# Five PSUM banks for the expert combines, and the last expert's rows taken out one expert earlier, in an encoder layer with 16 experts

## The chip, the cores and the metric

The kernel runs on one core of a Trainium2 chip. The metric is device time in microseconds for one execution of the whole layer. Before: 973.5 us, the median of three runs (973.33 to 974.92).

Five engines work beside each other, each in its own order: TensorE (matmuls; PE in the profile, and PEld for its weight loads), VectorE (DVE), ScalarE (ACT), GpSimd (POOL) and SyncE (SP), which issues nearly all transfers. TensorE writes into PSUM, which has eight banks; a 128x512 float32 tile fills one.

## What is computed

One encoder layer on 512 tokens of width 1024. Three attention branches, gated and merged, give `x` after a first layer norm. The change touches only what follows:

```python
    logits = jnp.einsum('btd,de->bte', x, w_router, preferred_element_type=jnp.float32)
    aff = jax.nn.softmax(logits, axis=-1)
    gate, idx = lax.top_k(jnp.swapaxes(aff, 1, 2), cap)          # 16 experts, cap = 64 tokens each
    xs = x[bidx, idx]
    h = jnp.einsum('becd,edf->becf', xs, w_gate_up)              # 1024 -> 2 x 1024
    hg, hu = jnp.split(h, 2, axis=-1)
    ye = jnp.einsum('becf,efd->becd', jax.nn.silu(hg) * hu, w_down)
    ye = ye * gate[..., None].astype(ye.dtype)
    ffn = jnp.zeros_like(x).at[bidx, idx].add(ye)
    x = layer_norm(DN_ALPHA * x + ffn, ln2_g[l], ln2_b[l])
```

Each expert picks 64 of the 512 tokens; a token can be picked by several experts, and the layer norm of a token needs the sum of all of them.

## The kernel before

**Weights.** An expert has 8 slots of gate and up weights, written gu(e,k), and 4 slots of down weights, dn(e,k), each 1 MiB. `Ring` fixes their order: gu(e,0..3), dn(e-1,0..3), gu(e,4..7), and for the last two experts gu(e,0), dn(e-1,0..3), gu(e,1..7); dn(15,0..3) comes last. SyncE issues a slot's transfer (L783; L781 for a tag of two separate tiles, and for the last slot) as soon as a buffer is free; with 24 buffers some 20 MiB can lie ahead of TensorE. A few buffers aren't reused late in the stage (`ONCE`, `LEAVE`).

**One expert.** `gate_up` (L1212) multiplies the 64 gathered tokens by a slot: two halves of g and two of u, 8 matmul records of 128x512 a slot. g and u fill a PSUM bank each, of the tags S and T, which have two banks each. `act_h` computes h from them: a tanh on ScalarE (L1220), two products on VectorE (L1221, L1222). `h_transpose` turns h with four transposes (L1228) and a copy (L1231), `products` (L1240) multiplies by the four dn slots, 32 matmul records, into the one bank of the tag Y, and `hi_lo` splits the result (L86 on ScalarE, L87 on VectorE). The order is written out by hand in the loop over `e` at the end: while expert e's gu slots run, expert e-1 is transposed and multiplied. After an odd expert `gather` collects the tokens of the next two.

**The accumulator.** `acc_of(m)` holds the sum for token tile m (128 tokens, m = 0 to 3) in SBUF. `combine(pr)` adds the two experts of pair pr: per tile and half of the width a pair of matmuls with the one-hot matrix (L1317, L1318) into one of the three banks of the tag mm, and an addition on VectorE (L1325); the third and sixth are first copied out by ScalarE (L1322) and added later (L1311). It runs within experts 3, 5, ..., 13 and, for pair 6, within expert 14, seven times.

**The last two experts.** Within expert 15, `Rows` handles expert 14. `slots` (L1389) makes its one-hot matrix, `down` its products, and `combine(m)` adds them to tile m (L1403, L1405) and takes the row sums along; a mean on GpSimd (L1407) and squares on ScalarE (L1409) follow. `take(m)` (L1413) then picks the rows that expert 15 needs out of the finished accumulator into a bank `fin`, of the tag S. `centre` (L1417), `spread` (L1420, L1421), the reciprocal square root (L94, L95, L99 to L101) and `finish` (L1426, L1427) normalise all rows on VectorE and send them out. Expert 15's own products go into `fin` on top of the taken rows, and `last_rows` normalises these 64 rows (two halves of the width on 128 partitions) and sends them with an indirect transfer (L1449) over the rows that were written before. `last_own` works out, in expert 14, which rows these are (L1365 and L1368 on VectorE, L1372 on TensorE, L1374).

`keep_warm(n)` issues n matmuls whose result nobody reads. `PB(tag, name)` gives the next bank of a tag.

Of the kernel before, what the change touches and what calls it, by code (L numbers as in the profile page):

```python
# [18 lines left out]
P = 128  # L19
# [23 lines left out]
def layer_kernel(ctx: ExitStack, tc: tile.TileContext, xt, xn, first0, wu, bgate, rpb, gains, wrt,  # L43
# [14 lines left out]
    def R(tag, shape, name, dt=F32, bufs=None):  # L58
        return rp.tile(shape, dt, name=name, tag=tag, bufs=bufs)

    PS_BUFS = {"mm": 3, "S": 2, "T": 2, "Y": 1}

    class Halves:
        def __init__(self, a, b):
# [11 lines left out]
    def RH(tag, name, dt=F32R):  # L76
        return Halves(*(R(tag + c, [P, 4, S], name + c, dt) for c in "ab"))

    def PB(tag, name, shape=(P, 512)):
        return ps.tile(list(shape), F32, name=name, tag=tag, bufs=PS_BUFS[tag])  # L80

    def small(shape, name, dt=F32, bufs=2):
# [620 lines left out]
    class Attn:  # L703
# [4 lines left out]
        def add(self, us):  # L708
            self.units += us
# [353 lines left out]
    def all_of(g):  # L1063
        for _ in g:
            pass
# [1 line left out]
    def then(*fs):  # L1067
        return lambda: [f() for f in fs]

    def keep_warm(n):  # L1070
        warm2 = PB("T", "warm2")
        for _ in range(n):
            nc.tensor.matmul(warm2[:, :P], ident, ident, start=True, stop=True)

# [128 lines left out]
    def gate_up(e, ks):  # L1203
        pr, i = divmod(e, 2)
        if ks[0] == 0:
            GU[e] = (PB("S", f"g{e}"), PB("T", f"u{e}"))
        for k in ks:
            w = ring.get("gu", e, k)
            xs = XS[pr][:, k, i * CAP:(i + 1) * CAP]
            for b in range(2):  # L1210
                for hf in range(2):
                    nc.tensor.matmul(GU[e][b][hf * 64:hf * 64 + 64], xs,  # L1212
                                     w[b][:, hf * 512:hf * 512 + 512],
                                     start=(k == 0), stop=(k == KD - 1))
            ring.done("gu", e, k)

    def act_h(e):
        g, u = GU.pop(e)
        HT[e] = th = R("t", [P, 512], f"h{e}")
        nc.scalar.activation(th, g, AF.Tanh, scale=0.5)  # L1220
        nc.vector.scalar_tensor_tensor(th, th, 1.0, g, op0=ALU.add, op1=ALU.mult)  # L1221
        nc.vector.scalar_tensor_tensor(th, th, GW[e // 2][:, e % 2:e % 2 + 1], u, op0=ALU.mult, op1=ALU.mult)  # L1222

    def h_transpose(e):
        h = HT[e]
        tp = PB("mm", f"ht{e}", (P, 4, P))
        for c in range(4):
            nc.tensor.transpose(tp[:, c], h[:, c * P:(c + 1) * P], ident)  # L1228
        t = R("tmp", [P, 4, P], f"hT{e}", bufs=2)
        HT[e] = t  # L1230
        nc.vector.tensor_copy(t, tp)  # L1231

    def products(e, y, first):
        hT = HT.pop(e)
# [66 lines left out]
                    yield  # L1301
            yield

    def combine(pr):
        yh, yl = YP.pop(pr)
        g = GT.pop(pr)
        later = []

        def catch_up():
            a, t = later.pop()  # L1310
            nc.vector.tensor_tensor(a, a, t, op=ALU.add)  # L1311

        for i in range(2 * NT):
            m, o = divmod(i, 2)
            c = slice(o * 512, (o + 1) * 512)
            cb = PB("mm", f"cb{pr}{m}{o}")
            nc.tensor.matmul(cb, g[:, m], yh[:, c], start=True, stop=False)  # L1317
            nc.tensor.matmul(cb, g[:, m], yl[:, c], start=False, stop=True)  # L1318
            a = acc_of(m)[:, c]
            if i in (2, 5):  # L1320
                t = R("t", [P, 512], f"cbs{pr}{i}")
                nc.scalar.copy(t, cb)  # L1322
                later.append((a, t))
            else:
                nc.vector.tensor_tensor(a, a, cb, op=ALU.add)  # L1325
            if i == 3:
                catch_up()
        catch_up()

    E = NEXP - 1  # L1330
    HALVES = [(slice(o * 64, o * 64 + 64), slice(o * 512, o * 512 + 512)) for o in range(2)]
# [31 lines left out]
    def last_own():  # L1363
        own, half, base = OH[E // 2][:, :, CAP:], ST["half"], ST["base"]
        nc.vector.tensor_copy(ST["pick"], own)  # L1365
        code = late_small(2, F16)
        for m in range(NT):
            nc.vector.tensor_scalar(code[:, m:m + 1], base, 8.0, 2.0 * m - 8.0, op0=ALU.mult, op1=ALU.add)  # L1368
        at = PB("mm", "rowat")
        for r, _ in HALVES:  # L1370
            for m in range(NT):
                nc.tensor.matmul(at[r, :1], own[:, m], code[:, m:m + 1], start=(m == 0), stop=(m == NT - 1))  # L1372
        ST["rowat"] = late_small(1, I32)
        nc.vector.tensor_tensor(ST["rowat"], at[:, :1], half, op=ALU.add)  # L1374

    class Rows:
# [6 lines left out]
        def slots(self):  # L1383
# [6 lines left out]
            self.g = R("tmp", [P, NT, P], "GTe", F32R, bufs=2)  # L1390
            nc.scalar.copy(self.g, gp)

        def down(self):
            y = PB("Y", f"y{E - 1}")
            products(E - 1, y, True)
            self.yy = R("lo", [P, 2, D], "ye", F32R)[:, 0]
            for r, c in HALVES:
                hi_lo(self.yy[0:64, c], self.yy[64:128, c], y[r])

        def combine(self, m):  # L1400
            for o, (_, c) in enumerate(HALVES):
                cb = PB("mm", f"cbe{m}{o}")
                nc.tensor.matmul(cb, self.g[:, m], self.yy[:, c], start=True, stop=True)  # L1403
                a = acc_of(m)[:, c]
                nc.vector.scalar_tensor_tensor(a, a, 1.0, cb, op0=ALU.mult, op1=ALU.add, accum_out=self.sums[:, o, m:m + 1])  # L1405
            nm = self.nm[:, m:m + 1]
            nc.gpsimd.tensor_scalar(nm, self.sums[:, 0, m:m + 1], self.sums[:, 1, m:m + 1], -1.0 / D, op0=ALU.add, op1=ALU.mult)  # L1407
            for o, (_, c) in enumerate(HALVES):
                nc.scalar.activation(ST["junk"], acc_of(m)[:, c], AF.Square, bias=nm, accum_out=self.sq[:, o, m:m + 1])  # L1409

# [17 lines left out]

    def last_rows():
        fin = ST["fin"]  # L1430
        t, d = PB("T", "lastst")[:, :2], PB("Y", "lastd")[:, :1]
        nc.tensor.matmul(t, ST["pair"], ST["eps2"], start=True, stop=False)
        products(E, fin, False)
        st, mv = late_small(6), late_small(2)
# [22 lines left out]
    for e in range(NEXP):  # L1457
# [5 lines left out]
        elif e < NEXP - 2:  # L1463
# [4 lines left out]
            for k in range(4):  # L1468
                if k == 3:
                    h_transpose(e - 1)  # L1470
                    if e % 2 and e > 1:
                        combine((e - 3) // 2)
                gate_up(e, (k,))
                steps(side, side)
            if e == 12:
# [10 lines left out]
        elif e == NEXP - 2:  # L1486
            gate_up(e, (0,))
            h_transpose(e - 1)
            down(e - 1)
            rows = Rows()  # L1490
            rows.slots()
            last_own()
            gate_up(e, (1, 2))
            combine(e // 2 - 1)
            gate_up(e, tuple(range(3, KD)))
        else:
            gate_up(e, (0,))
            h_transpose(e - 1)
            rows.down()
            gate_up(e, (1,))  # L1500
            ST["fin"] = PB("S", "fin")
            for m in range(NT):
                rows.combine(m)
                gate_up(e, (m + 2,))
                rows.take(m)
            for m in range(NT):
                rows.centre(m)
            gate_up(e, (6, 7))
        act_h(e)
        if e % 2 and e < NEXP - 1:  # L1510
            all_of(gather(e // 2 + 1))
    rows.spread()
    h_transpose(NEXP - 1)
    rsqrt_steps(rows.y, rows.hv, rows.a)
    for m in range(NT):
        rows.finish(m)
    warm_s = late_small(1)
# [115 lines left out]
```

## Time and profile before

| what | us |
|---|---|
| median of three runs | 973.5 |
| the profiled execution, its own time | 975.0 |
| its span, from the first to the last instruction | 973.2 |
| its mean granted TensorE clock | 0.988 |
| first weight matmul of expert 0 | at 526.8 |
| combine of pair 5, in expert 13 | from 864.1 |
| last products, of expert 15 | from 956.0 |

A row of the timeline gives the start (us from the start of the span), the length, the engine, the line, the operation, what it writes and reads, the shape and the number of instructions merged into it; in brackets stands how long the engine had been idle before it, and what ended that. Matmuls are pipelined: their rows overlap, and a matmul's own pace is read from the distance of starts. A row of the groups gives line, engine, operation and tiles, the count, the busy time and the mean length in ns. In a row of the windows view the granted clock is 1.00 at full speed and 0.50 at half.

### The profile page before, as it was taken

How to read it: one execution, taken by the hardware profiler on the slowest of the kernel's cores; microseconds unless marked ns; L12 is line 12 of the kernel's file. 1: busy time of each engine (PE TensorE's matmuls, PEld its weight loads, DVE VectorE, ACT ScalarE, POOL GpSimd, SP SyncE). 2: the span in 40 equal slices, each digit the busy share in tenths (PEclk: the TensorE clock that was granted, in tenths of full speed). 3: DMA queues.
4: the chain of work that ended last, by engine and by line, in shares of the span. 5: the costliest groups of instructions: out<-in, count | busy, mean ns of one | idle time of the engine just before them, and what ended most of it. 6: DMA issues, size and time to landing. Idle time of an engine off the chain costs nothing.

```text
span 973.2 us, 13726 instructions
## 1 busy us (share of the span) xinstructions
PE 943.3 (97%) x5510; PEld 615.8 (63%) x5510; DVE 453.7 (47%) x885; ACT 289.0 (30%) x593; POOL 94.2 (10%) x115
## 2 busy tenths in 40 slices
PE   8999999999999999999999999999999999999895
PEld 8899877889888888888887343434343343434332
DVE  6347678665275666335464165223141323232336
ACT  5343344444344444334232011111020111211121
POOL 0102303000031221006022000000000000000000
PEclk9999999999999999999999999999999999999898
DMA  9322211111343332584849999999999999999992
GB/s 356 110 66 66 65 45 64 60 50 44 91 122 94 112 93 69 181 305 176 311 161 408 426 407 426 424 427 425 426 424 427 426 426 424 427 424 427 424 409 101
DMA packets 53119, 251.88 MB, mean 259 GB/s; under 512 B 14176, under 2 KB 14592, under 8 KB 30656
## 3 DMA queue, kind: packets, MB, share of 16 engines
q1 hardware_dynamic: 52832, 250.23, 65.0%
q8 instruction: 43, 0.70, 0.3%
q10 hardware_dynamic: 144, 0.52, 0.1%
q0 software_dynamic: 80, 0.26, 0.1%
q14 instruction: 20, 0.16, 0.0%
HBM read 247.84 MB, written 2.36 MB: 257 GB/s over the span
## 4 chain that ended last, share of the span: by engine, by line
PE 86%; DVE 6%; ACT 3%; POOL 2%; issue 1%; DMA 1%; SPq 0%; POOLq 0%; ACTq 0%; DVEq 0%
PE g L1212 12%; PE u L1212 11%; PE y L1240 11%; PE gate L254 4%; PE gate L255 4%; PE gate L256 4%; PE pr L254 2%; PE pr L255 2%; PE pr L256 2%; PE ga L1181 2%; PE nqk L254 1%; PE nqk L256 1%; PE nqk L255 1%; PE gy L609 1%; PE ga L1183 1%
## 5 line engine op out<-in xcount | busy, mean ns | idle before, releaser
L1212 PE MATMUL g<-gu,xs 128*64 128x512 f32 x512 | 135.9, 608 | 0.0
L1212 PE MATMUL u<-gu,xs 128*64 128x512 f32 x512 | 133.2, 597 | 0.0
L1240 PE MATMUL y<-dn,hT 128*64 128x512 f32 x480 | 105.7, 593 | 2.1 <-DVE hT L1231 2.1
L1212 PEld LDWEIGHTS u<-gu,xs 128*64 128x64 f32 x512 | 37.9, 138 | 73.7 <-issue 72.8
L87 DVE TENSOR_TENSOR lo_twin<-raw_twin,whi 128x1024 fp32r<-128x1024 f32 x43 | 54.2, 1260 | 54.1 <-ACT whi L86 53.9
L1240 PEld LDWEIGHTS y<-dn,hT 128*64 128x64 f32 x480 | 34.2, 137 | 70.3 <-issue 64.5
L87 DVE TENSOR_TENSOR y<-y,y 64x512 fp32r<-64x512 f32 x28 | 19.3, 689 | 122.8 <-ACT y L86 122.8
L86 ACT CAST whi<-raw_twin 128x1024 fp32r<-128x1024 f32 x64 | 67.3, 1051 | 17.4 <-PE wo L1022 8.7
L1212 PEld LDWEIGHTS g<-gu,xs 128*64 128x64 f32 x512 | 33.7, 137 | 55.2 <-issue 52.0
L86 ACT CAST y<-y 64x512 fp32r<-64x512 f32 x28 | 16.2, 579 | 175.3 <-PE y L1240 164.8
L87 DVE TENSOR_TENSOR wlo<-raw_twin,whi 128x1024 fp32r<-128x1024 f32 x21 | 27.5, 1311 | 39.1 <-ACT whi L86 39.0
L1407 POOL TENSOR_SCALAR rp<-rp 128x1 f32<-128x1 f32 x4 | 2.0, 510 | 426.2 <-DVE acc L1405 426.2
L254 PE MATMUL gate<-xha,whi 128*128 128x512 f32 x96 | 38.9, 405 | 0.0
L1231 DVE COPY hT<-ht 128x512 f32<-128x512 f32 x16 | 11.1, 691 | 59.4 <-PE ht L1228 59.4
L255 PE MATMUL gate<-xla,whi 128*128 128x512 f32 x96 | 37.5, 390 | 0.0
L254 PE MATMUL gate<-xhb,whi 128*128 128x512 f32 x96 | 37.3, 389 | 0.0
L255 PE MATMUL gate<-xlb,whi 128*128 128x512 f32 x96 | 37.3, 389 | 0.0
L1221 DVE SCALAR_TENSOR_TENSOR h<-h,g 128x512 f32<-128x512 f32 x16 | 11.0, 688 | 56.4 <-ACT h L1220 56.4
L585 ACT ACTIVATE P_twin<-gs,nm 128x512 f32<-128x512 f32 x32 | 21.7, 683 | 52.4 <-DVE nm L584 52.4
L1325 DVE TENSOR_TENSOR acc<-acc,cb 128x512 f32<-128x512 f32 x42 | 27.5, 683 | 10.6 <-PE cb L1318 10.6
L256 PE MATMUL gate<-xha,lo_twin 128*128 128x512 f32 x80 | 31.2, 390 | 0.0
L628 POOL TENSOR_TENSOR bm<-bf,hm 128x256 f32<-128x256 f32 x24 | 18.8, 820 | 127.3 <-DMA bf<-in_rpb 122.3
(426 smaller groups left out, 2017.7 us busy)
## 6 DMA issues: line engine op xcount, KB each, us to landing
gu<-in_wgu SPq DMA_DIRECT2D x115, 1024.0 KB
dn<-in_wdn SPq DMA_DIRECT2D x58, 1024.0 KB
raw_twin<-in_wu SPq DMA_DIRECT2D x65, 512.0 KB
gu<-in_wgu SPq DMA_DIRECT2D x26, 512.0 KB
dn<-in_wdn SPq DMA_DIRECT2D x12, 512.0 KB
raw<-in_wu SPq DMA_DIRECT2D x8, 512.0 KB
xr<-in_xt SPq DMA_DIRECT2D x4, 512.0 KB
x<-in_xn SPq DMA_DIRECT2D x2, 1024.0 KB
```

Of the source, the lines that this page charges most:

```text
L86: nc.scalar.copy(hi, src)
L87: nc.vector.tensor_tensor(lo, src, hi.bitcast(F32), op=ALU.subtract)
L254: nc.tensor.matmul(acc, w_h, rh[:, k], start=(k == 0), stop=False)
L255: nc.tensor.matmul(acc, w_h, rl[:, k], start=False, stop=False)
L256: nc.tensor.matmul(acc, w_l, rh[:, k], start=False, stop=(k == nk - 1))
L585: nc.scalar.activation(self.p[:, h], self.s[h], AF.Exp, bias=nm[:, h:h + 1], accum_out=self.sm[:, h:h + 1])
L628: nc.gpsimd.tensor_tensor(bm[:, h, ty].rearrange("p (b r c) -> p r b c", b=4, r=8), bf[:, h, :, 16 - 8 * ty:48 - 8 * ty].rearrange("p r (b ...
L1181: nc.tensor.matmul(g, XH[:, m, c], oh[:, m], start=(m == 0), stop=False)
L1212: nc.tensor.matmul(GU[e][b][hf * 64:hf * 64 + 64], xs, w[b][:, hf * 512:hf * 512 + 512], start=(k == 0), stop=(k == KD - 1))
L1231: nc.vector.tensor_copy(t, tp)
L1240: nc.tensor.matmul(y[o * 64:o * 64 + 64], hT[:, c, hf * 64:hf * 64 + 64], w[j][:, o * 512:(o + 1) * 512], start=(first and k == 0 and j == ...
L1325: nc.vector.tensor_tensor(a, a, cb, op=ALU.add)
```

## The change

There are four edits.

- The tags S and T become S0, S1, T0 and T1 with one bank each. `PB` alternates between the two by itself, or takes the one that is asked for: expert e's g and u lie in the banks of index e % 2, except g of expert 15, which lies in S0. `combine` puts its fourth and fifth result into the S and T banks that the running expert doesn't use, and all eight results are added on VectorE straight out of PSUM.
- `last_own` stops before its matmuls; they run later in expert 14, after the combine and one slot more. The rows for expert 15 are taken out of the accumulator within expert 14, between its last four slots, when expert 14's own part isn't in it yet. That part is added in expert 15: `match` multiplies the one-hot matrices of experts 14 and 15 into a 64x64 matrix that says which of their slots hold the same token, and `add` multiplies expert 14's result by it into `fin`.
- In expert 15 the mean moves from GpSimd to VectorE, the centring of tiles 0 and 1 into the loop, and `spread` and the reciprocal square root from behind the expert to ahead of its last two slots.
- At the end come 6 dummies ahead of the last transposes and 2 behind them. The last h is finished in two halves, and its transposed copy is shared by ScalarE and VectorE.

```diff
-    PS_BUFS = {"mm": 3, "S": 2, "T": 2, "Y": 1}
+    PS_BUFS = {"mm": 3, "S0": 1, "S1": 1, "T0": 1, "T1": 1, "Y": 1}
...
-    def PB(tag, name, shape=(P, 512)):
+    turn = {"S": 0, "T": 0}
+
+    def PB(tag, name, shape=(P, 512), ix=None):
+        if tag in turn:
+            if ix is None:
+                ix = turn[tag]
+                turn[tag] = 1 - ix
+            tag += str(ix)
         return ps.tile(list(shape), F32, name=name, tag=tag, bufs=PS_BUFS[tag])
...
-    def keep_warm(n):
-        warm2 = PB("T", "warm2")
+    def keep_warm(n, bank="T"):
+        warm2 = PB(bank, "warm2")
...
         if ks[0] == 0:
-            GU[e] = (PB("S", f"g{e}"), PB("T", f"u{e}"))
+            GU[e] = tuple(PB(t, f"{n}{e}", ix=0 if e == NEXP - 1 and t == "S" else e % 2) for t, n in (("S", "g"), ("T", "u")))
...
-            for b in range(2):
+            for b in (1, 0) if (e, k) == (NEXP - 1, 0) else (0, 1):
...
-        nc.vector.scalar_tensor_tensor(th, th, GW[e // 2][:, e % 2:e % 2 + 1], u, op0=ALU.mult, op1=ALU.mult)
+        for c in (slice(0, 256), slice(256, 512)) if e == NEXP - 1 else (slice(0, 512),):
+            nc.vector.scalar_tensor_tensor(th[:, c], th[:, c], GW[e // 2][:, e % 2:e % 2 + 1], u[:, c], op0=ALU.mult,
+                                           op1=ALU.mult)
...
-        nc.vector.tensor_copy(t, tp)
+        if e == NEXP - 1:
+            nc.scalar.copy(t[:, 0:2], tp[:, 0:2])
+            nc.vector.tensor_copy(t[:, 2:4], tp[:, 2:4])
+        else:
+            nc.vector.tensor_copy(t, tp)
...
-    def combine(pr):
+    def combine(pr, other):
...
-            cb = PB("mm", f"cb{pr}{m}{o}")
+            cb = PB({3: "S", 4: "T"}.get(i, "mm"), f"cb{pr}{m}{o}", ix=other)
             nc.tensor.matmul(cb, g[:, m], yh[:, c], start=True, stop=False)
             nc.tensor.matmul(cb, g[:, m], yl[:, c], start=False, stop=True)
             a = acc_of(m)[:, c]
-            if i in (2, 5):
-                t = R("t", [P, 512], f"cbs{pr}{i}")
-                nc.scalar.copy(t, cb)
-                later.append((a, t))
-            else:
-                nc.vector.tensor_tensor(a, a, cb, op=ALU.add)
-            if i == 3:
-                catch_up()
-        catch_up()
+            nc.vector.tensor_tensor(a, a, cb, op=ALU.add)
...
             nc.vector.tensor_scalar(code[:, m:m + 1], base, 8.0, 2.0 * m - 8.0, op0=ALU.mult, op1=ALU.add)
+        yield
         at = PB("mm", "rowat")
...
+        def match(self):
+
+            both = R("lo", [P, 2, D], "ye", F32R)
+            self.yy, self.same = both[:, 0], both[:, 1, :CAP]
+            mp = PB("mm", "same")[:, :CAP]
+            oh = OH[E // 2]
+            for r, _ in HALVES:
+                for m in range(NT):
+                    nc.tensor.matmul(mp[r], oh[:, m, :CAP], oh[:, m, CAP:], start=(m == 0), stop=(m == NT - 1))
+            nc.scalar.copy(self.same, mp)
+
+        def add(self):
+            for r, c in HALVES:
+                nc.tensor.matmul(ST["fin"][r], self.same.bitcast(F32), self.yy[:, c].bitcast(F32), start=False, stop=False)
...
-                cb = PB("mm", f"cbe{m}{o}")
+                cb = PB("T" if (m, o) == (1, 1) else "mm", f"cbe{m}{o}", ix=0)
...
-            nc.gpsimd.tensor_scalar(nm, self.sums[:, 0, m:m + 1], self.sums[:, 1, m:m + 1], -1.0 / D, op0=ALU.add, op1=ALU.mult)
+            nc.vector.tensor_scalar(nm, self.sums[:, 0, m:m + 1], self.sums[:, 1, m:m + 1], -1.0 / D, op0=ALU.add, op1=ALU.mult)
...
             rows.slots()
-            last_own()
+            side = last_own()
+            steps(side)
             gate_up(e, (1, 2))
-            combine(e // 2 - 1)
-            gate_up(e, tuple(range(3, KD)))
+            combine(e // 2 - 1, (e + 1) % 2)
+            gate_up(e, (3,))
+            all_of(side)
+            ST["fin"] = PB("S", "fin", ix=1)
+            for m in range(NT):
+                gate_up(e, (4 + m,))
+                rows.take(m)
         else:
             gate_up(e, (0,))
+            rows.match()
             h_transpose(e - 1)
             rows.down()
             gate_up(e, (1,))
-            ST["fin"] = PB("S", "fin")
             for m in range(NT):
                 rows.combine(m)
+                if m > 1:
+                    rows.centre(m - 2)
                 gate_up(e, (m + 2,))
-                rows.take(m)
-            for m in range(NT):
+            for m in (2, 3):
                 rows.centre(m)
+            rows.spread()
+            rsqrt_steps(rows.y, rows.hv, rows.a)
+            rows.add()
             gate_up(e, (6, 7))
...
-    rows.spread()
+    keep_warm(6, "mm")
     h_transpose(NEXP - 1)
-    rsqrt_steps(rows.y, rows.hv, rows.a)
+    keep_warm(2, "mm")
     for m in range(NT):
         rows.finish(m)
```

More of the change, by code (lines that the diff above doesn't have):

```diff
@@ L1302, in residual @@
             yield
-    def combine(pr):
+    def combine(pr, other):
         yh, yl = YP.pop(pr)
         g = GT.pop(pr)
[L1307 to L1311, printed above, removed]
         for i in range(2 * NT):
@@ L1395, in down @@
             products(E - 1, y, True)
-            self.yy = R("lo", [P, 2, D], "ye", F32R)[:, 0]
             for r, c in HALVES:
@@ L1430, in last_rows @@
         fin = ST["fin"]
-        t, d = PB("T", "lastst")[:, :2], PB("Y", "lastd")[:, :1]
+        t, d = PB("T", "lastst", ix=0)[:, :2], PB("Y", "lastd")[:, :1]
         nc.tensor.matmul(t, ST["pair"], ST["eps2"], start=True, stop=False)
@@ L1471, in layer_kernel @@
                     if e % 2 and e > 1:
-                        combine((e - 3) // 2)
+                        combine((e - 3) // 2, (e + 1) % 2)
                 gate_up(e, (k,))
```

## Prediction, made before the changed kernel was run

> **What bounds the kernel now.** First the page, parts 1, 2 and 5: who is busy, and in which stage.
>
> ```profile
> span 973.2 us, 13726 instructions
> PE 943.3 (97%) x5510; PEld 615.8 (63%) x5510; DVE 453.7 (47%) x885; ACT 289.0 (30%) x593; POOL 94.2 (10%) x115
> ...
> GB/s 356 110 66 66 65 45 64 60 50 44 91 122 94 112 93 69 181 305 176 311 161 408 426 407 426 424 427 425 426 424 427 426 426 424 427 424 427 424 409 101
> ```
>
> TensorE is the busy engine, but in the expert stage (from slice 22 on) the transfers also run without a break at about 425 GB/s: 1 MiB every 2.47 us. There are thus two clocks: TensorE's own pace, and the weight stream, which can't run faster. A slot of weights takes TensorE 1.72 us, so TensorE eats the stream's lead up. How much lead is left is seen where it is smallest, in the last slot of expert 13, gu(13,7). The TensorE timeline there, and the DMA view of the stretch 878.95 to 958 us (before the first output leaves):
>
> ```profile
> 883.46 1.03 PE L1212 MATMUL g<-gu,xs 128*64 128x512 f32 x4
> 884.32 1.03 PE L1212 MATMUL u<-gu,xs 128*64 128x512 f32 x4
> 885.28 0.40 PE L1181 MATMUL ga<-oh,xA 128*128 128x128 f16 x4
> ...
> 889.29 1.08 PE L1212 MATMUL g<-gu,xs 128*64 128x512 f32 x4
> ...
> q1 hardware_dynamic: 4472, 29.36, 88.4%
> ```
>
> After gu(13,7) the ring's order has 28 slots left: gu(14,0), four dn, seven gu, gu(15,0), four dn, seven gu, four dn. 28 x 1.0486 MB is 29.36 MB, so gu(13,7) had landed at 878.95. TensorE took it at 883.46 (the last weight matmuls ahead of the gather at 885.28): a lead of 4.5 us. **Whatever is won before this point counts up to 4.5 us and no further.** Behind it the gather, which needs no weights, gives lead back.
>
> **The combine.** TensorE, ScalarE and VectorE at expert 13, on the timeline:
>
> ```profile
> 864.12 0.48 PE L1317 MATMUL cb<-y,GT 128*128 128x512 f32 x1
> ...
> 865.01 1.27 DVE L1325 TENSOR_TENSOR acc<-acc,cb 128x512 f32<-128x512 f32 x2
> ...
> 867.13 0.39 PE L1317 MATMUL cb<-y,GT 128*128 128x512 f32 x1
> ...
> 867.60 0.39 PE L1317 MATMUL cb<-y,GT 128*128 128x512 f32 x1
> ...
> 868.53 0.50 PE L1317 MATMUL cb<-y,GT 128*128 128x512 f32 x1 [0.31 <-ACT cbs L1322]
> ...
> 869.19 1.08 PE L1212 MATMUL g<-gu,xs 128*64 128x512 f32 x4
> ```
>
> From the first matmul to the next weights: 5.07 us. A pair that waits for no bank takes 0.47 (867.13 to 867.60); eight are 3.76, with 0.2 for the changes of shape 3.95. Do five banks keep it so? VectorE starts 0.9 after the first matmul and clears a bank per 0.64. With the transposes ahead holding one bank, pairs 6, 7 and 8 want the banks of pairs 1, 2 and 3 at 2.5, 3.0 and 3.5; they are free at 1.55, 2.2 and 2.8. So nothing waits: **1.1 us saved per combine**, bounded by 0 (the banks never were the limit) and 1.3. VectorE has eight additions as before (six and two late ones); the two ScalarE copies go. The two borrowed banks are those of expert e-1, whose readers ended before its transposes could start, and expert e+1 wants them over 10 us later. Six such combines (experts 3 to 13) offer 6.6 us by gu(13,7); the stream allows 4.5 less the delay from landing to use. That delay no row of before shows for a load, because nothing waits at the edge. The nearest is an output, from the chain of waits:
>
> ```profile
> 962.58 2.79 DMA out<-acc
> ```
>
> 0.5 MiB at 425 GB/s are 1.23 of the 2.79, so the notice costs 0 to 1.56; I take 0.3, near the low end, since an output also has its start-up in that row while these loads follow one another in a full queue. **Term 1: -4.2 us** (-2.9 to -4.5); the other 2.4 us become short waits of TensorE for the stream within expert 13's slots. The Trainium skill (DMA: Bandwidth & Descriptors, Anatomy of one DMA) gives about 2.0 us of fixed cost per transfer, most of it the receipt after the last byte; with all of it behind the landing, term 1 would by its figure be an estimated -2.5, and no row of before shows such a wait for a load.
>
> **Expert 14.** Its TensorE timeline, and two stretches of the windows view (columns: length, then busy time of PE, PEld, DVE, ACT, POOL, granted clock, DMA share, GB/s):
>
> ```profile
> 892.60 0.65 PE L1240 MATMUL y<-dn,hT 128*64 128x512 f32 x2 [0.78 <-DVE hT L1231]
> ...
> 899.52 0.39 PE L1389 MATMUL gTe<-id,oh 128*64 128x128 f16 x8
> 902.80 0.40 PE L1372 MATMUL rowat<-rp,oh 128*64 128x1 f16 x5 [2.89 <-DVE rp L1368]
> ...
> 906.48 2.10 PE L1212 MATMUL g<-gu,xs 128*64 128x512 f32 x4
> ...
> 909.68 0.50 PE L1317 MATMUL cb<-y,GT 128*128 128x512 f32 x1
> ...
> 914.65 1.08 PE L1212 MATMUL g<-gu,xs 128*64 128x512 f32 x4
> ...
> 926.54 7.09 PE L1240 MATMUL y<-dn,hT 128*64 128x512 f32 x32 [0.78 <-DVE hT L1231]
> 933.45 1.03 PE L1212 MATMUL g<-gu,xs 128*64 128x512 f32 x4
> ...
> 897.80:902.20 4.40, 2.11 (x18) 0.78 (x14) 1.21 (x2) 1.68 (x3) 0.00 (x0) 1.00 1.00 425
> 903.20:909.00 5.80, 5.80 (x17) 2.78 (x17) 0.16 (x1) 0.00 (x0) 0.00 (x0) 0.50 1.01 425
> ```
>
> The row-number matmuls (L1372) hold TensorE for 2.89 us behind VectorE, and after that gap the granted clock is 0.50 for 6 us. Moved behind the combine and gu(14,3), they find VectorE's part long done. I add up the new path from gu(14,0) to gu(15,1), 44.16 before (889.29 to 933.45): to the products 3.31; products 6.92; slots 0.43; two slots at full clock 3.5; combine 4.0; one slot 1.8; row numbers 0.35; four slots 6.9; the four takes, moved here, 3.7 (0.86 of matmul each, row below, and a little); gu(15,0) 1.7; the match matrix 0.45 (eight half-precision matmuls like L1389's); transposes and copy 1.44; products 6.91. Sum 41.4: **term 2: -2.8 us** (the bounds -2.3 to -3.3 are the small new pieces). gu(14,1) to gu(15,1) all lie 0.7 us or more behind their landing at 2.47 a slot. A new wait: g of expert 15 now shares a bank with g of expert 14, so all TensorE work queues behind ScalarE's tanh and one VectorE product (1.3 us by the rows of the next part). u goes first, and with take(3) ahead that is 1.7 us of cover: nothing.
>
> **Expert 15.** TensorE and VectorE, timelines:
>
> ```profile
> 938.56 1.03 PE L1413 MATMUL fin<-acc,last 128*64 128x512 f32 x4
> 939.52 0.73 PE L1403 MATMUL cbe<-ye,GTe 128*128 128x512 f32 x2
> 940.18 1.08 PE L1212 MATMUL g<-gu,xs 128*64 128x512 f32 x4
> ...
> 940.05 0.69 DVE L1405 SCALAR_TENSOR_TENSOR acc<-acc,cbe 128x512 f32<-128x512 f32 x1 [2.41 <-PE cbe L1403]
> ...
> 948.05 4.88 DVE L1417 SCALAR_TENSOR_TENSOR acc<-acc,rp,ln2row 128x1024 f32<-128x1024 f32 x4
> 953.00 0.69 DVE L1221 SCALAR_TENSOR_TENSOR h<-h,g 128x512 f32<-128x512 f32 x1
> 953.79 0.75 DVE L1222 SCALAR_TENSOR_TENSOR h<-h,gw,u 128x512 f32<-128x512 f32 x1
> ...
> 955.89 0.16 DVE L99 TENSOR_TENSOR rp<-rp 128x4 f32<-128x4 f32 x1
> ...
> 957.68 4.87 DVE L1426 SCALAR_TENSOR_TENSOR acc<-acc,rp,ln2row 128x1024 f32<-128x1024 f32 x4
> ```
>
> Times from gu(15,1). Without the takes a step of the loop is 0.66 + 1.77 + 0.1 = 2.53 instead of 3.39, so with the add (two matmuls like a take, 0.86) TensorE ends its weights at 17.1, not 19.7. But **VectorE becomes the bound.** The third combine reaches it at 8.3 (PE at 7.75 and 0.53 for the matmul, 939.52 to 940.05). From there, in order: four accumulations 2.45, their readouts 0.16, two means 0.4 (moved from POOL), four centrings 4.88, and thirteen small steps at 0.2 (nine take 955.89 to 957.68) 2.6. Only then, at 18.8, may it multiply h, which ScalarE has had ready since 17.0; before it was 19.55 (953.00). Then 0.8 for the product, 0.4 for the first half of the next, two transposes, 0.35 for half a copy on ScalarE; the other half, two dummies and the bias matmul end at about 21.35. Before, the last products started at 22.58 (956.03 in the next part). **Term 3: -1.2 us**; -2.8 without VectorE's lateness, 0 if every small step took 0.3.
>
> **The end.** TensorE and the windows:
>
> ```profile
> 954.59 0.66 PE L1228 MATMUL ht<-ident,h 128*128 128x128 f32 x4 [1.41 <-DVE h L1222]
> ...
> 956.03 8.78 PE L1240 MATMUL fin<-dn,hT 128*64 128x512 f32 x32 [0.67 <-DVE hT L1231]
> ...
> 957.00:960.20 3.20, 3.20 (x10) 0.97 (x8) 3.06 (x7) 0.00 (x0) 0.00 (x0) 0.50 0.12 50
> ```
>
> The last products take 8.78 for 7.09 elsewhere (926.54), because the clock halves after the gaps. Six dummies last 1.4 and two 0.5 (22 dummy matmul records last 2.70 at 510.69, two to a dummy):
>
> ```profile
> 510.69 2.70 PE L1073 MATMUL warm<-ident 128*128 128x128 f32 x22
> ```
>
> They cover 17.1 to 18.5; a gap of 1.4 stays until the transposes. Before, 1.41, the transposes and 0.67 were enough for a drop, so holding isn't certain; I take it as held: **term 4: -1.7 us** (0 to -1.7). The Trainium skill (TensorE: Matmul & The Clock Gate, Why this matters for your kernels) puts a drop only behind idle gaps over about 3 us; by it this gap is harmless, while the rows above show a drop after shorter ones. The four output steps (4.87) run beside the products' 7.1, and the last weights land before 950, so what follows the products, 8.4 us to the end, moves with them unchanged.
>
> **Sum.** -4.2 - 2.8 - 1.2 - 1.7 = -9.9. The profiled execution took 975.0 (973.2 span and 1.8 around it), so 965.1 on its scale; it lies 1.5 above the median of the timed runs, 973.5, and on that scale the forecast is **963.6 us**.
>
> **Rivals.** (a) The clock drops at the end all the same: term 4 goes, 965.3. For it: the remaining gap beside the rows above; against it: 1.9 us of dummies in the stretch. (b) The landing notice is late, by 1.6 as bounded above: TensorE leaves expert 13 later, 964.9. (The 2.0 us of the Trainium skill's page named there would make it 965.3.) (c) Five banks don't do what they say, because the order of the evacuations and not their number holds TensorE: term 1 is nothing and term 2 loses 1.1, 968.9. Against it, the sole releasers in the combine are bank readers. (d) VectorE isn't late in expert 15 because its small steps overlap: 962.0. (e) Slower than before: at the stream's edge TensorE works 1.72 of each 2.47 us; if gaps of 0.75 lowered the clock, each such drop would cost 1.6 (half of 3.2, as at 957.0), and from six drops among experts 13 to 15 the gain is eaten; eight would give about 976. Against it: 897.80 to 902.20 shows a drop only after TensorE was busy for less than half of a stretch.
>
> **How the numbers follow.** Chances: forecast 0.48, (a) 0.22, (b) 0.10, (c) 0.05, (d) 0.08, (e) 0.03, and 0.04 for smaller losses between 966 and 972. Forecast, (a), (b) and most of (d) make over 0.8; their ends are (d) with its 0.5 of unknown pieces, 961.5, and (a) with (b), 966.6, with 0.4 of the same pieces: range **961.5 to 967.0**. A measurement can tell about 0.2% (2 us) from no change: faster 0.95, within it 0.02, slower 0.03.
>
> **What would show it.** Combine 3.9 to 4.0 long with no wait on a reader; PE waits for weights in gu(13,5) to gu(13,7), and gu(13,7) taken within 0.5 us of 879; no clock of 0.5 near expert 14; g product of expert 15 waiting not for tanh but behind VectorE's small steps; last products in 7.1. A stream ending much before or after 949 us would move term 1 by as much.

## The result, and the profile after

| what | before | after |
|---|---|---|
| median of four runs each, us | 973.4 (973.1 to 974.9) | 963.2 (962.4 to 965.2) |
| ratio, 95% interval | | 0.990 (0.988 to 0.991) |
| the profiled execution, its own time | 975.0 | 965.2 |
| its span | 973.2 | 963.5 |
| first gate product of expert 0, gu(0,0) | 526.84 | 526.26 |
| from gu(0,0) to gu(13,7) | 356.6 | 354.4 |
| from gu(13,7) to gu(14,0), the gather | 5.8 | 5.9 |
| from gu(14,0) to gu(15,1) | 44.2 | 40.4 |
| from gu(15,1) to the last products | 22.6 | 21.0 |
| the last products | 8.8 | 7.1 |
| from their end to the end of the span | 8.4 | 8.5 |

The lower part of the table is made of starts on the TensorE timeline. Its differences are the 9.7 us between the spans: 0.6 ahead of gu(0,0), where no edit acts, then 2.2, 3.8, 1.6 and 1.7, less 0.2 for the gather and what follows the products. The forecast was 963.6. First the page of the changed kernel: span, busy time, transfers.

```profile
span 963.5 us, 13754 instructions
...
PE 938.5 (97%) x5538; PEld 618.5 (64%) x5538; DVE 452.5 (47%) x890; ACT 281.5 (29%) x581; POOL 91.3 (9%) x111
...
GB/s 360 111 67 67 60 51 66 46 65 32 100 123 98 85 83 110 147 298 188 306 175 358 428 415 418 424 427 425 426 426 425 427 425 426 426 426 424 428 424 243
```

The stream runs as before, without a break and at the same 425 GB/s. What changed is how close TensorE comes to it. Its timeline at expert 13's combine and at gu(13,7), and the line of the waits that belongs to the weights (total, times, longest):

```profile
860.77 0.48 PE L1324 MATMUL cb<-y,GT 128*128 128x512 f32 x1
861.09 0.39 PE L1325 MATMUL cb<-y,GT 128*128 128x512 f32 x1
...
864.43 0.39 PE L1325 MATMUL cb<-y,GT 128*128 128x512 f32 x1
864.75 1.08 PE L1219 MATMUL g<-gu,xs 128*64 128x512 f32 x4
...
878.24 1.08 PE L1219 MATMUL u<-gu,xs 128*64 128x512 f32 x4
880.65 1.08 PE L1219 MATMUL g<-gu,xs 128*64 128x512 f32 x4 [1.33 <-DMA gu<-in_wgu]
```

```profile
PE g L1219 <- DMA gu<-in_wgu: 3.1, 5, 1.3
```

The combine takes 3.98 us (860.77 to 864.75) where it took 5.07, and no matmul of it waits for a reader of a bank. Six of them give 6.5 us, but gu(13,7) starts only 2.2 us earlier. The other 4.3 are the five waits for weights: 3.1 idle, and after each wait some 0.2 in which the pipeline fills. TensorE meets the stream at gu(12,7), gu(13,0), gu(13,1) and gu(13,2), and once more at gu(13,7). When had gu(13,7) landed? By the same count as in the prediction (28 slots, 29.36 MB, are left), in the DMA view of the stretch 878.45 to 949.4:

```profile
q1 hardware_dynamic: 4469, 29.34, 98.4%
```

By this count it had landed at about 878.4, and TensorE got to use it at 880.65, **2.2 us later**. (The count goes by the starts of packets; by their ends it is 1.9.) The prediction had allowed 0.3. But the chain view of the stretch 860 to 882, in order of time, has the load end at 880.61:

```profile
865.87 14.74 DMA gu<-in_wgu
880.61 0.04 issue
880.65 1.08 PE g L1219 x4
```

Why do the two differ? The 16 DMA engines share every load, and each reports its own share: a load leaves 16 counts on its semaphore (the counter that TensorE waits for). For gu(13,7) the trace has them from 877.08 to 880.61, at 878.90 in the mean. Each stands some 0.3 us behind a four-byte packet, and that packet directly behind a packet of data. So the report itself is quick, and the engines are out of step by 3.5 us. A count of bytes adds all engines up and so finds the landing of the mean engine; the slot can be used when the last engine is through. TensorE starts 0.04 us after its report. In the kernel before, the same records have gu(13,7) complete at 880.91, not at 878.95, so the lead there was 2.5 us and not 4.5.

Expert 14 and expert 15, on the timelines of TensorE and VectorE:

```profile
886.54 1.08 PE L1219 MATMUL g<-gu,xs 128*64 128x512 f32 x4
...
896.77 0.39 PE L1389 MATMUL gTe<-id,oh 128*64 128x128 f16 x8
896.99 1.03 PE L1219 MATMUL g<-gu,xs 128*64 128x512 f32 x4
...
906.16 0.29 PE L1372 MATMUL rowat<-rp,oh 128*64 128x1 f16 x8
906.28 1.08 PE L1219 MATMUL g<-gu,xs 128*64 128x512 f32 x4
...
918.33 0.32 PE L1401 MATMUL same<-oh 128*64 128x64 f16 x8
918.58 0.66 PE L1237 MATMUL ht<-ident,h 128*128 128x128 f32 x4
...
926.93 1.03 PE L1219 MATMUL g<-gu,xs 128*64 128x512 f32 x4
...
944.08 1.61 PE L1080 MATMUL warm<-ident 128*128 128x128 f32 x12
946.58 0.83 PE L1237 MATMUL ht<-ident,h 128*128 128x128 f32 x4 [0.89 <-DVE h L1230]
...
947.90 7.09 PE L1253 MATMUL fin<-dn,hT 128*64 128x512 f32 x32
```

```profile
939.38 3.67 DVE L1431 SCALAR_TENSOR_TENSOR acc<-acc,rp,ln2row 128x1024 f32<-128x1024 f32 x3
942.97 0.16 DVE L1434 TENSOR_TENSOR rp<-rp 128x4 f32<-128x4 f32 x1
...
945.17 0.17 DVE L108 SCALAR_TENSOR_TENSOR rp<-rp 128x4 f32<-128x4 f32 x1
945.25 0.68 DVE L1228 SCALAR_TENSOR_TENSOR h<-h,g 128x512 f32<-128x512 f32 x1
```

The row numbers cost 0.12 us (906.16 to 906.28) and no wait; the matrix of same tokens 0.25 (918.33 to 918.58). In expert 15, h's first product stands directly behind VectorE's thirteen small steps, with no idle time in brackets: VectorE is the bound there. The last products run at full clock.

In what follows a kernel's **end** is the end of its span less the start of its gu(0,0). In the 14 profiles of this study gu(0,0) starts between 523.2 and 526.9 us, though nothing ahead of it is edited, so spans don't compare to 2 us and ends do: 446.35 before, 437.21 after. The timed medians carry that spread too: the kernel before had medians of 971.5 to 971.6 in the three later batches of runs.

### The profile page after: what moved, and what is told of

It reads as the page before. It is cut to its first block, busy times and chain, and to the rows that moved or that the text cites. A ratio compares the mean times of both kernels' runs of the same rounds, so it can differ in the third digit from the quotient of the medians.

```text
span 963.5 us, 13754 instructions
## 1 busy us (share of the span) xinstructions
PE 938.5 (97%) x5538; PEld 618.5 (64%) x5538; DVE 452.5 (47%) x890; ACT 281.5 (29%) x581; POOL 91.3 (9%) x111
## 4 chain that ended last, share of the span: by engine, by line
PE 81%; DMA 6%; DVE 6%; ACT 2%; POOL 2%; issue 1%; SPq 0%; POOLq 0%; DVEq 0%; ACTq 0%
PE g L1219 10%; PE u L1219 9%; PE y L1253 9%; PE gate L261 4%; PE gate L263 4%; PE gate L262 4%; DMA gu<-in_wgu 3%; PE pr L261 2%; DMA dn<-in_wdn 2%; PE pr L262 2%; PE pr L263 2%; PE ga L1188 2%; PE nqk L263 2%; PE nqk L262 2%; PE nqk L261 2%; PE gy L616 1%
## 5 line engine op out<-in xcount | busy, mean ns | idle before, releaser
L1327 DVE TENSOR_TENSOR acc<-acc,cb 128x512 f32<-128x512 f32 x56 | 34.0, 679 | 1.1 <-PE cb L1325 1.1
L1227 ACT ACTIVATE h<-g 128x512 f32<-128x512 f32 x16 | 9.6, 597 | 77.1 <-PE g L1219 77.1
```

## The experiments

Each is the changed kernel with one edit, where nothing else is said. The first four ask what limits TensorE at gu(13,7): the stream, with a slot usable 2.2 us after the count of bytes (6.5 us offered, 2.2 taken), the stream with the prediction's 0.3 us (4.2 taken), or no stream at all (every 1.1 comes through).

**1. Only the combine of expert 14 has five banks**; those of experts 3 to 13 run as before, with three banks and two copies on ScalarE.

```diff
+        five = pr in (6,)
...
-            cb = PB({3: "S", 4: "T"}.get(i, "mm"), f"cb{pr}{m}{o}", ix=other)
+            cb = PB({3: "S", 4: "T"}.get(i, "mm") if five else "mm", f"cb{pr}{m}{o}", ix=other)
...
-            nc.vector.tensor_tensor(a, a, cb, op=ALU.add)
+            if not five and i in (2, 5):
+                t = R("t", [P, 512], f"cbs{pr}{i}")
+                nc.scalar.copy(t, cb)
+                later.append((a, t))
+            else:
+                nc.vector.tensor_tensor(a, a, cb, op=ALU.add)
...
```

> The changed kernel, but the six combines of experts 3 to 13 as before the change (three banks, two ScalarE copies); the one in expert 14 keeps five banks. Theory S (the weight stream is the edge, and a slot can be used about 2 us after its last packet): the changed kernel got only 2.2 us out of these six combines, so this is 2.2 us slower than the changed kernel, about 965.4 us, and gu(13,7) is taken without a wait for its weights. Theory P (as predicted, usable 0.3 us after landing): 4.2 slower, 967.4. Theory N (no edge, every combine counts with 1.1): 6.5 slower, 969.7.

Measured: end 439.26, 2.05 later, and no wait for weights; median 965.4, ratio 0.995 (0.993 to 0.997). Its combine, on the TensorE timeline:

```profile
865.62 0.50 PE L1331 MATMUL cb<-y,GT 128*128 128x512 f32 x1 [0.31 <-ACT cbs L1336]
```

The six combines together are worth 2 us, not 4.2 and not 6.5.

**2. Five banks for the combines of experts 3, 5, 7 and 14** (the same edit, with `five = pr in (0, 1, 2, 6)`).

> The changed kernel, but only the combines of experts 3, 5, 7 (and 14) with five banks; those of 9, 11, 13 as before. Theory S: three combines win 3.3 us up to gu(13,7), more than the 2.2 that the stream lets through, so nothing is lost: 963.2 us as the changed kernel, with a shorter wait for gu(13,7) (about 0.3 us instead of 1.3). Theory N: 3.3 slower, 966.5.

Measured: end 437.46, 0.25 later; median 965.1, ratio 0.993 (0.992 to 0.995). The waits:

```profile
PE g L1219 <- DMA gu<-in_wgu: 1.0, 2, 0.6
```

With half of the combines fast, all but 0.25 us of the gain is there, and the waits for weights shrink from 3.1 to 1.0. The later three combines buy waits. Even the 0.25 is no loss of the combines: TensorE waits for gu(13,7) in both kernels, and here its last report came 0.3 later after gu(0,0).

**3. One slot less in the stream**: gu(8,1) is not loaded, and TensorE multiplies by gu(8,0) a second time in its place, so its work stays and 1 MiB of transfer goes.

```diff
+            if key in SHARED:
+                mate = self.order[i - 1]
+                self.t[key] = self.t[mate]
+                self.tag[key] = self.tag.pop(mate)
+                self.n += 1
+                return
...
```

> The changed kernel with one transfer of 1 MiB left out: gu(8,1) is not loaded, expert 8 uses the weights of gu(8,0) twice. Every matmul stays. Theory S: the stream behind it lands 2.45 us earlier, and so the time falls by 2.4 us to about 960.8. If the waits in expert 13 are not the stream's: 963.2.

Measured: end 434.19, 3.0 earlier; median 961.1, ratio 0.990 (0.988 to 0.991). Some 2.5 are the slot. The rest came unasked: the buffers rotate, so that gu(13,7) fell into a buffer of two separate tiles, which is loaded by two transfers, and TensorE could begin on the first. It began 1.1 us after the count for the whole slot, not 1.9 (both by packet ends). That gave experiment 8.

**4. Four slots less**: the same for gu(6,1), gu(7,1), gu(8,1) and gu(9,1).

> As with one transfer less, but four: gu(6,1), gu(7,1), gu(8,1), gu(9,1) are not loaded, and the slot before each is used twice. The stream is then 9.8 us earlier. Theory S: the waits before gu(13,7), 4.3 us in all, vanish and no more, since TensorE is then the bound: about 958.9. If the stream sets the end throughout: 953.4. If it never does: 963.2.

Measured: end 432.84, 4.4 earlier; median 959.3, ratio 0.988 (0.986 to 0.990). TensorE at gu(13,6) and gu(13,7):

```profile
872.88 1.03 PE L1228 MATMUL u<-gu,xs 128*64 128x512 f32 x4
873.73 1.03 PE L1228 MATMUL g<-gu,xs 128*64 128x512 f32 x4
874.59 1.03 PE L1228 MATMUL u<-gu,xs 128*64 128x512 f32 x4
```

No wait is left, and gu(13,7) starts 4.3 us earlier than in the changed kernel, which is just what its waits had cost. With 10 us less of stream nothing more is to be had: TensorE is then alone the bound. So in the changed kernel the stream takes 4.3 of the 6.5 us, and the size of that share is set by the engine that reports last.

**5. Without the dummies at the end.**

```diff
-    keep_warm(6, "mm")
     h_transpose(NEXP - 1)
-    keep_warm(2, "mm")
```

> The changed kernel without the 6 and 2 dummies. Theory D (the clock drops when TensorE does little for about 3.4 us, and the dummies prevent it): the gap before the last products is 3.8 us with 0.7 us of transposes in it, so the last products take about 8.8 us instead of 7.1 in this profile, and the time is 0.5 to 1.7 us above the changed kernel's 963.2, as the drop meets a part of the runs. Rival (the shorter gap alone holds the clock, the dummies do nothing): products 7.1, time the same or 0.2 shorter, since two dummies stand ahead of the products.

Measured: end 437.55, 0.3 later; median 965.1, ratio 0.994 (0.992 to 0.996). The stretch up to the last products and that of the products, in the windows view:

```profile
943.00:947.20 4.20, 1.48 (x10) 0.67 (x6) 2.93 (x13) 0.68 (x2) 0.00 (x0) 1.00 0.81 336
947.20:954.00 6.80, 6.73 (x32) 2.21 (x32) 5.21 (x5) 1.50 (x3) 0.00 (x0) 1.00 0.72 294
```

TensorE was busy for a third of 4.2 us, and the clock stayed up all the same. In this execution the dummies were not needed. The 0.3 us are no cost of the missing dummies either: gu(13,7) already starts 0.4 later after gu(0,0), because its last report did.

**6. The kernel before with five banks and nothing else.**

```diff
-    PS_BUFS = {"mm": 3, "S": 2, "T": 2, "Y": 1}
+    PS_BUFS = {"mm": 3, "S0": 1, "S1": 1, "T0": 1, "T1": 1, "Y": 1}
...
-            combine(e // 2 - 1)
+            combine(e // 2 - 1, (e + 1) % 2)
```

> The kernel before with the five banks alone: own banks for S0, S1, T0, T1, eight additions on VectorE straight from PSUM; experts 14 and 15 and the end as before. Theory S: 2.2 us by gu(13,7), then 1.1 in the combine of expert 14, so 3.3 faster than before, and from the first weight matmul to the end 443.1 instead of 446.4. If every combine counted: 7.6 faster, 438.8.

Measured: end 440.83, 5.5 earlier than before; median 967.3, ratio 0.996 (0.994 to 0.997). gu(13,7) starts 1.5 earlier and the combine of expert 14 takes 1.1 less. Why 1.5 and not 2.2? The mean report of gu(13,7) came as in the changed kernel, 352.7 us after gu(0,0), but the last one 0.7 later. The rest is clock: the last products took 7.09 with no edit near them, and the half clock in expert 14 lasted one stretch of 3.4 us, not 6.8. TensorE's timeline at the end, and the windows view in expert 14:

```profile
949.16 0.66 PE L1235 MATMUL ht<-ident,h 128*128 128x128 f32 x4 [1.41 <-DVE h L1229]
...
950.61 7.09 PE L1247 MATMUL fin<-dn,hT 128*64 128x512 f32 x32 [0.67 <-DVE hT L1238]
```

```profile
900.50:903.90 3.40, 3.40 (x11) 1.77 (x9) 0.00 (x0) 0.00 (x0) 0.00 (x0) 0.51 1.02 429
903.90:908.00 4.10, 4.10 (x20) 2.64 (x17) 1.90 (x4) 0.00 (x0) 0.00 (x0) 0.99 1.01 426
```

The gaps of 1.41 and 0.67 ahead of the last products are those of the kernel before to the digit; there the clock fell, here it did not.

**7. The reciprocal root's steps behind the last product of h.**

```diff
             rows.spread()
-            rsqrt_steps(rows.y, rows.hv, rows.a)
             rows.add()
...
+    rsqrt_steps(rows.y, rows.hv, rows.a)
     keep_warm(6, "mm")
```

> The changed kernel with the nine steps of the reciprocal square root (1.8 us of VectorE) moved from ahead of the last h to behind it. Theory V (VectorE's small steps hold up the last h by 1.3 us): the last products start 1.3 us earlier, 1.3 us faster than the changed kernel, about 961.9; from the first weight matmul to the end 435.9 instead of 437.2. Rival (something else holds h, or what is won is lost because the copy of h then waits for the steps): 963.2 and 437.2.

Measured: end 435.91, 1.3 earlier; median 962.8, ratio 0.991 (0.989 to 0.993). VectorE's timeline:

```profile
940.80 0.17 DVE L102 TENSOR_SCALAR rp<-rp 128x4 f32<-128x4 f32 x1
941.32 0.69 DVE L1228 SCALAR_TENSOR_TENSOR h<-h,g 128x512 f32<-128x512 f32 x1 [0.35 <-ACT h L1227]
```

Now VectorE waits 0.35 for the tanh, and the way from gu(15,1) to the last products is 19.69 us, not 20.97. The loss that the prediction charged to VectorE is there.

**8. The slots at the stream's edge as two transfers each.** L781 and L783 of the kernel before choose between two transfers and one; gu(13,7), gu(14,1) and gu(14,2) now take two.

```diff
-            if tag in PAIRED or i == len(self.order) - 1:
+            if tag in PAIRED or i == len(self.order) - 1 or key in SPLIT:
```

> The changed kernel with gu(13,7), gu(14,1), gu(14,2) loaded as two transfers of 0.5 MiB each. Theory S: g of gu(13,7) needs the first half only, which lands 1.2 us earlier; u then waits for the second half, so TensorE is 0.8 us ahead behind it: 962.4, and 436.4 from the first weight matmul to the end. If the waits in expert 13 come from elsewhere: 963.2 and 437.2.

Measured: end 436.36, 0.85 earlier; median 963.6, ratio 0.992 (0.990 to 0.994). TensorE at gu(13,7), and the DMA view of the stretch 875.1 to 945.7:

```profile
874.78 1.08 PE L1220 MATMUL u<-gu,xs 128*64 128x512 f32 x4
876.03 1.08 PE L1220 MATMUL g<-gu,xs 128*64 128x512 f32 x4 [0.17 <-DMA gu<-in_wgu]
877.27 1.08 PE L1220 MATMUL u<-gu,xs 128*64 128x512 f32 x4 [0.16 <-DMA gu<-in_wgu]
```

```profile
q1 hardware_dynamic: 4789, 29.35, 99.2%
```

By the count the whole slot had landed at 875.1, its first half 1.23 (0.5 MiB at 425 GB/s) earlier, at 873.9. TensorE starts on that half at 876.03, again 2.2 us after the count, and on the second half 1.24 later. The last reports of the halves come at 875.99 and 877.23, and the 16 reports of each spread over 3.4 us: the distance between the engines does not shrink with the transfer. gu(13,7) starts 1.5 us earlier than in the changed kernel. Of these 0.2 go into the wait for its second half, and 0.5 at the second half of gu(14,2), where TensorE meets the stream again:

```profile
895.56 1.08 PE L1220 MATMUL u<-gu,xs 128*64 128x512 f32 x4 [0.20 <-DMA gu<-in_wgu]
```

**9. Both edits, 7 and 8, together.**

> The changed kernel with both of the last edits together: the three slots at the edge of the stream as two transfers each, and the reciprocal-root steps behind the last product of h. If the two act at different places (the landing of the last weight; VectorE's small steps in expert 15) the gains add: -0.85 and -1.3, so the end 435.1 us after the first gate product where the changed kernel has 437.2, about 2.1 us less time than it. Rival: they share one limit (a weight that is used earlier makes VectorE no earlier): only the larger counts, 435.9.

Measured: end 435.36; median 961.6 (960.2 to 962.5), ratio 0.990 (0.988 to 0.992), beside 964.2 of the changed kernel on the same chip. The ends differ by 1.85 from 437.21 and by 1.95 from experiment 10, so the two gains of 1.3 and 0.85 nearly add. (The split's share is made otherwise: gu(13,7) starts only 0.8 earlier here, as the last engine was 2.2 behind the mean and not 1.5, but nothing is lost at gu(14,2).) This version is faster than both kernels, by 2.6 and 10.0 us in the medians of this chip.

**10. The changed kernel once more.**

> The changed kernel itself once more, on the chip of this batch, as the measure for the others: the end 437.2 us after the first gate product if the place of the end does not vary with the run, and about 0.990 of the kernel before. If the clock's drop at the end comes and goes with the run, 437.2 in one run and some 1.7 us more in another.

Measured: end 437.31; median 964.2, ratio 0.993 (0.991 to 0.995). The end repeats to 0.1 us, but not step by step: gu(13,7) starts 0.4 earlier, and then TensorE waits for gu(14,2), which costs 0.5:

```profile
898.23 1.08 PE L1219 MATMUL g<-gu,xs 128*64 128x512 f32 x4 [0.29 <-DMA gu<-in_wgu]
```

In this batch the gain is 7.4 us by medians where the first measurement gave 10.2: the changed kernel moved by 1.0 and the kernel before by 1.8.

**11. The kernel before with the row numbers later.**

```diff
+        yield
         at = PB("mm", "rowat")
...
-            last_own()
+            side = last_own()
+            steps(side)
             gate_up(e, (1, 2))
             combine(e // 2 - 1)
-            gate_up(e, tuple(range(3, KD)))
+            gate_up(e, (3,))
+            all_of(side)
+            gate_up(e, tuple(range(4, KD)))
```

> The kernel before with one order changed: the products that make the row numbers of the last expert stand behind the combine and the third gate product of expert 14, so that TensorE does not stand waiting for them. Theory (the wait in expert 14 costs its own length and starts the half clock): the gap of 2.9 us goes, and with it up to 3.2 us of half clock: from gu(14,0) to gu(15,0) 33.99 us becomes 31.1 without the clock's part and about 27.9 with it. Rival (the five slots of expert 14 and what was moved are short of work elsewhere): under 1 us.

Measured: 27.74 us from gu(14,0) to gu(15,0) where the kernel before took 33.99; end 440.17, 6.2 earlier; median 966.8, ratio 0.996 (0.994 to 0.997). The row numbers, on TensorE's timeline, and in the windows view that place and the end:

```profile
907.40 0.29 PE L1373 MATMUL rowat<-rp,oh 128*64 128x1 f16 x8
907.52 1.08 PE L1212 MATMUL g<-gu,xs 128*64 128x512 f32 x4
```

```profile
899.00:903.00 4.00, 4.00 (x19) 1.85 (x14) 2.57 (x9) 1.21 (x3) 0.00 (x0) 1.00 1.01 428
...
944.00:947.80 3.80, 1.72 (x12) 0.95 (x12) 3.26 (x12) 1.68 (x3) 0.00 (x0) 1.00 0.48 197
947.80:951.20 3.40, 3.40 (x12) 0.96 (x10) 3.19 (x8) 0.00 (x0) 0.00 (x0) 0.50 0.06 25
```

One order changed takes out the wait of 2.9 and, with it, the half clock behind it (1.00 in the first row), 3.3 us more. At the end, with the same gaps as in experiment 6 and TensorE busy for 1.72 of 3.80 us, the clock did fall here, and the last products took 8.78.

**12. The kernel before with the dummies alone.**

```diff
+    keep_warm(6)
     h_transpose(NEXP - 1)
+    keep_warm(2)
```

> The kernel before with the 6 and 2 dummy products around the last transposes and nothing else. Theory (they keep the clock up): the last 32 products take 7.1 us in place of 8.78, -1.7 us. Rival (whether a window of low clock falls on the last products hangs on where the windows begin in a run): the products take 7.1 or 8.8 with the dummies as without, and the median moves by less than 1 us.

Measured: median 969.8 of twelve runs, ratio 0.999 (0.997 to 1.000); last products 7.09.

```profile
952.22 7.09 PE L1240 MATMUL fin<-dn,hT 128*64 128x512 f32 x32 [0.22 <-DVE hT L1231]
```

End 443.33, 3.0 earlier: 1.7 the products, 1.3 the half clock in expert 14, which again lasted one stretch of 3.4 us, with nothing changed there. By the medians the dummies are worth 1.8 us, by the interval between 2.6 us and nothing.

## Why the prediction was right, and where it was not

The time came as forecast, 963.2 against 963.6, but not term by term: one term was 2.0 us too large, two were 1.0 and 0.4 too small, and 0.6 came from ahead of the experts. That these nearly cancel is luck. So is a part of the profile's 9.7 us: the kernel before was caught with the clock low for long in expert 14 and again at the end. That is 1.3 and 1.7 us which experiment 6, with the same orders in both places, does not have.

**Term 1, the combines: -4.2 forecast, -2.2 measured.** The 1.1 us per combine held, and so did the mechanism, a lead of the stream that caps what they bring (experiments 2 and 4). The step that failed is the size of the lead, 4.5 us. It was read from a count of bytes, as if a slot were there when its share of the bytes had moved. In the kernel before, the mean report of gu(13,7) came 0.5 after that count and the last one another 1.5 later, so the real lead was 2.5. The delay of 0.3 from landing to use, which the prediction thought its doubtful number, is about right for one engine: some 0.3 us from its last data to its report, and 0.04 from the last report to TensorE. In us from gu(0,0), for gu(13,7), in the kernel before and in those that load the whole stream and wait there:

| kernel | mean of the 16 reports | last report | TensorE starts |
|---|---|---|---|
| before (no wait) | 352.59 | 354.07 | 356.62 |
| changed | 352.64 | 354.35 | 354.39 |
| 2, five banks to expert 7 | 352.76 | 354.68 | 354.73 |
| 5, no dummies | 352.84 | 354.72 | 354.76 |
| 6, five banks alone | 352.67 | 355.06 | 355.11 |
| 7, steps after h | 352.64 | 354.32 | 354.36 |
| 8, first half of the slot | 351.32 | 352.83 | 352.87 |
| 9, first half of the slot | 351.41 | 353.58 | 353.62 |
| 10, changed once more | 352.53 | 353.92 | 353.97 |

The mean of a whole slot stays within some 0.3 us, the last report is 1.4 to 2.4 behind it, and TensorE follows the last report wherever it waits. A fixed delay of the report would keep the distance from the mean the same; it does not. Rival (b), a late notice, thus had nearly the right size (2.2 by the prediction's own count, above its bound of 1.56) for another reason. The Trainium skill (DMA: Bandwidth & Descriptors, Anatomy of one DMA) puts about 2.0 us of fixed cost on a transfer, most of it the receipt after the last byte; it says so for transfers that GpSimd issues. These loads, issued by SyncE, do not show it: 1.7 of the 2.2 us are the distance from the mean engine to the last, and the report takes some 0.3. What the prediction called short waits of TensorE for the stream, 2.4 us, came as 4.3, and four of the five came earlier than the slots that it had named, gu(13,5) to gu(13,7).

**Term 2, expert 14: -2.8 forecast, -3.8 measured.** The mechanism holds: experiment 11 gets 6.2 us from moving the row numbers alone; in the changed kernel the takes that moved into this expert use part of them up. The small new pieces were taken too dear: the one-hot matrix of expert 14 0.22 for 0.43, the combine 3.87 for 4.0, the row numbers 0.12 for 0.35, the match 0.25 for 0.45, and the four slots with the takes and gu(15,0) 12.05 for 12.3. All were priced by the lengths of rows; rows overlap, and a piece in a full pipeline costs the distance of starts. That gu(14,1) to gu(15,1) lie 0.7 us or more behind their landing held in this profile and not in all: experiments 8 and 10 wait at gu(14,2). Part of this term hangs on the run: the half clock behind the wait lasted 6.8 us in one profile of that order and 3.4 in two, a difference of 1.3.

**Term 3, expert 15: -1.2 forecast, -1.6 measured.** VectorE is late by its small steps, as the prediction said against its rival (d): h's first product came at 18.3 after gu(15,1) (forecast 18.8), and experiment 7 gets 1.3 back by moving nine of them. The thirteen steps take 2.3, not 2.6 (942.97 to 945.25).

**Term 4, the clock at the end: -1.7 forecast, -1.7 measured in this pair of profiles.** But the cause is only half shown. In the ten profiles with dummies the last products took 7.09. In the four without them they took 8.78 twice (before, experiment 11) and 7.09 twice (experiments 5 and 6), with the same gaps ahead of them in three of the four. So without dummies the drop comes in some executions and not in others; that dummies always prevent it is likely from ten of ten, and the timed runs of experiments 5 and 12 fit a value between nothing and 1.8 us. How often the kernel before drops there wasn't measured, so the term's mean worth stays open.

**Rivals.** (a) and (c) did not occur in the profile, and (e) neither: with five waits at the edge of the stream no half clock followed. For that matter the prediction's argument, a drop only where TensorE was busy for less than half of a stretch, held in every profile shown; experiment 5 shows that it isn't enough for a drop.

## What to carry to other kernels

Where TensorE has caught up with a stream of weights, read the lead from the report of a load's last engine and not from a count of bytes, which was 2.2 us too early here. Cut the slots right at the edge into smaller transfers: a slot in halves can be begun half of its landing time earlier. A wait in which TensorE idles for 3 us can cost twice its length through the clock, so move what waits on another engine behind work that is ready, and put nothing small on VectorE ahead of the product that TensorE needs. Price small TensorE pieces by the distance of starts, and trust a gain of the clock only where several executions show it.

## What was not expected of the hardware

**The 16 DMA engines of a full stream run out of step.** In the 14 profiles the reports of one load in the late expert stage (840 to 945 us) spread over 3.0 to 5.2 us, for 1 MiB and for 0.5 MiB alike, while the stream as a whole moves 425 GB/s without a break. The four outputs of 0.5 MiB at the end of the changed kernel, with the stream over, spread over 0.2 us. The distance differs from run to run and can change within one (3.5 to 3.9 us in the changed kernel). What makes an engine fall behind was not tested.

**The clock falls by stretches of about 3.4 us that don't start with the gap.** After the same 1.41 and 0.67 us of gaps it fell in two profiles and stayed up in one; around one wait of 2.9 us it was half for 6.8 us once and for 3.4 twice. In the kernel before that wait lies at 899.91 to 902.80, and the clock is half from 902.26 to 909.09. The Trainium skill (TensorE: Matmul & The Clock Gate, Part 1: The HAM clock gate) describes a free-running window of about 3.4 us in which activity is counted; lengths and changes from run to run agree with that. Its rule to avoid idle gaps over about 3 us (Why this matters for your kernels, there) is not enough here: the rows of experiment 11 show a stretch of half clock behind a stretch with no single gap above 1.41.
